# Giving each unit of split weights its own starting position within 128 bytes of SBUF

## The chip, the cores and the metric

The kernel runs on one core of one Trainium2 chip. The metric is the device time of one execution in microseconds. Before the change the median of three runs is 904.43 us (904.04 to 904.75). The profile comes from one execution of its own, which took 903.08 us; its span, from the first to the last instruction, is 901.3 us.

## The reference, cut to what matters

A decoder trunk of two layers works on 256 tokens of width 1024. All of it is float32.

```python
for l in range(DEPTH):
    y = hybrid_mixer(x, w_in[l], ...)          # three attention branches, gates, output projection
    x = layer_norm(DN_ALPHA * x + y, ln_g[l, 0], ln_b[l, 0])
    y = memory_cross_attention(x, mem, xa_w_q[l], xa_w_kv[l], xa_w_o[l])
    x = layer_norm(DN_ALPHA * x + y, ln_g[l, 1], ln_b[l, 1])
    y = jnp.square(jax.nn.relu(x @ mlp_w_up[l])) @ mlp_w_down[l]
    x = layer_norm(DN_ALPHA * x + y, ln_g[l, 2], ln_b[l, 2])
```

Nearly all of the arithmetic is products of activations (256 rows) with weight matrices that are read once from HBM.

## The kernel before, in words

**Split products.** Every large product is made from three matmuls in the type float32r. Each operand is split into a high part and a low part, and `mm3` (line 316) adds high times high, low times high and high times low into one PSUM tile. So each piece of a weight is used three times, twice through its high half and once through its low half.

**The weight stream.** All weights lie in HBM as one stream of units, each 128 partitions by 1024 float32. `load_to` (line 242) fetches a unit by DMA into one of five `raw` buffers. `split_piece` (line 254) then splits it in two pieces of 512 columns: ScalarE writes the high half (`hi`, line 266), VectorE subtracts it from the raw weight and writes the low half (`lo`, line 267). `pump`, which is called from every `tick` of the matmul loop, keeps up to four units split ahead of the one in use.

**Where the halves lie.** Units of three groups (`t1`, `ut`, `mem`; the list `IN_PAGES`) get their halves as `phi` and `plo` from a pool of pages. All other units get `whi` and `wlo` from the pool `wp`, six buffers for each name. In the built program the `whi` buffers begin at byte 80192 of each partition and every 4096 bytes after it, the `wlo` buffers at 104768 and every 4096 bytes after it. The activations `xhi` and `xlo` begin at 16512 and 24704; the pool of pages begins at 141632 in steps of 4096, and that of half pages (`hh`, `hl` of the MLP among them) at 129344 in steps of 2048. Counted modulo 128 bytes, `xhi` and `xlo` and all their slices begin at 0; `whi`, `wlo`, the pages and the half pages, and all their slices that a matmul reads, begin at 64.

**How TensorE reads them.** A matmul has a stationary operand of 128 by 128, which a weight load brings in, and a moving operand of 256 or 512 columns. Both are read from SBUF, and the weight load for the next matmul runs while the present one streams. Three uses matter here:

- `f_tile` (line 326): the weights are stationary (slices of 128 columns), and 256 columns of activations move. Used for most of the input projection, the gates, the branch projections and the MLP's first product.
- `product` in `mlp` (line 1116): the activations `hh` and `hl` are stationary, and 512 columns of the weights `whi` and `wlo` move.
- `t_chunk` (line 582): as `product`, with 512 or 256 columns of weights moving, for `t1`, `t2`, `mix`, `ut`, `xq` and `xv`.

```python
    def f_tile(self, out, unit, xT, kt=KT, off=0, cols=P):
        self.mm3(out, [(tuple(u[:, off + k * P:off + k * P + cols] for u in unit),
                        tuple(x[:, k, :] for x in xT)) for k in range(kt)])
```

```python
        def product(p, k, tb, ch, t):
            self.mm3(acc[tb][ch], [(tuple(y[:, k, tb * P:(tb + 1) * P] for y in hs[p]),
                                    tuple(v[:, 512 * ch:512 * ch + 512] for v in t))],
```

The functions that the change touches:

Of the kernel before, what the change touches and what calls it, by code (L numbers as in the profile page):

```python
# [11 lines left out]
F32R = mybir.dt.float32r  # L12
# [8 lines left out]
P = 128  # L21
# [29 lines left out]
def stream_groups():  # L51
    per = [("t1", 2), ("t1", 2), ("misc", 1), ("fq", 2), ("fk", 2), ("t2", 2), ("t2", 2), ("uq", 2),
           ("nq", 2), ("nq", 2), ("ncv", 2), ("nk", 2), ("w1", 2), ("w1", 2)]
    for j in range(4):
        per += [("gmf", 2), ("gmf", 2), ("brmf", 1)]
    per += [("gn", 2)] * 4 + [("brn", 2)] * 2
    per += [("mix", 2)] * 2 + [("mem", 2)] + [("mix", 2)] * 2
    per += [("xk", 2), ("xq", 2), ("xv", 2), ("xo", 2)]
    per += [("ut", 2), ("ut", 2)]
    for p in range(2, 16):  # L60
        per += [("up", 2), ("dn", 2)]
    per += [("dn", 2)] * 2
    return per
# [124 lines left out]
class Halves:  # L188


    def __init__(self, tiles):
        self.tiles = tiles
# [5 lines left out]
def r(ap):  # L198
    return ap.bitcast(F32)
# [30 lines left out]
class Kernel:  # L230
    def __init__(self, tc, a, out, scratch):
        self.tc, self.nc, self.a, self.out, self.scr = tc, tc.nc, a, out, scratch
        self.groups = [(l, n, k) for l in range(L) for n, k in stream_groups()]
        self.offs = np.concatenate([[0], np.cumsum([k for _, _, k in self.groups])])
        self.units = [(i, k) for i, (_, _, n) in enumerate(self.groups) for k in range(n)]
        self.raws, self.halves = {}, {}
        self.gi = self.next_load = self.next_piece = 0
        self.mv = {}
        self.side, self.work = [Side() for _ in range(NSIDE)], 0.0


# [12 lines left out]
    def split_piece(self):  # L254

        u, c = divmod(self.next_piece, 1024 // SPL)
        self.next_piece += 1
        self.load_to(u)
        if c == 0:
            if self.paged(u):  # L260
                self.halves[u] = (self.page([P, 1024], F32R, "phi"), self.page([P, 1024], F32R, "plo"))
            else:
                self.halves[u] = tuple(self.wp.tile([P, 1024], F32R, name=n, tag=n) for n in ("whi", "wlo"))
        sl = (slice(None), slice(c * SPL, c * SPL + SPL))
        hi, lo = self.halves[u]
        self.nc.scalar.activation(hi[sl], self.raws[u][sl], AF.Copy)  # L266
        self.nc.vector.tensor_sub(lo[sl], self.raws[u][sl], r(hi[sl]))  # L267
# [913 lines left out]
```

## Time and profile before

| What | Value |
|---|---|
| median of three runs | 904.43 us |
| profiled execution | 903.08 us |
| its span | 901.3 us |
| outside the span | 1.8 us |
| TensorE (PE) busy | 877.9 us, 97% |
| weight loads (PEld) busy | 798.0 us, 89% |
| VectorE (DVE) busy | 643.7 us, 71% |
| ScalarE (ACT) busy | 540.9 us, 60% |
| GpSimd (POOL) busy | 52.8 us, 6% |
| mean DMA rate | 178 GB/s |

Matmuls are pipelined, and the end of one in the records is modelled. So the busy time of one matmul (some 280 ns for 256 columns) is not what it costs in a stream; that is the distance from its start to the start of the next, and it is read from the timeline, as the distance of two rows' starts divided by the number of matmuls between them. At the full clock of 2.4 GHz 256 columns at one column a cycle are 106.7 ns, and 512 columns are 213.3 ns.

### The profile page before, as it was taken

Reading aid. Unit: us, or ns where it says so; the run is one execution under the profiler, and the core shown is the slowest. Engines: PE = TensorE matmul, PEld = TensorE weight load, DVE = VectorE, ACT = ScalarE, POOL = GpSimd, SP = SyncE. Lnnn points to the kernel's source line nnn. Section 1 sums busy time; section 2 is a strip of 40 time slices with the busy share of each in tenths; the row PEclk is TensorE's granted clock in tenths of the full one; section 3 lists DMA queues with packets and bytes.
Section 4 is the critical chain, followed back from the end, with each engine's and each line's share of the span. In section 5 each row is a group of like instructions: output and inputs, shape, how many; then the busy total and the mean of one; then the engine's idle time right before and its main releaser. Section 6 shows DMA issues by size and latency. Waiting matters only on the chain.

```text
span 901.3 us, 16105 instructions
## 1 busy us (share of the span) xinstructions
PE 877.9 (97%) x6034; PEld 798.0 (89%) x6034; DVE 643.7 (71%) x1411; ACT 540.9 (60%) x1173; POOL 52.8 (6%) x114
## 2 busy tenths in 40 slices
PE   8999999999999999999999999999999999999996
PEld 6999899998877999999889999999988689999994
DVE  5888898768886555555776989886778845555554
ACT  6777967556683444555656777675567545555551
POOL 1000000001211000000130000000021300000002
PEclk9999999999999999999999999999999999999998
DMA  9854645547553566666645435554667446666631
GB/s 330 264 184 146 207 159 158 160 148 275 181 201 118 187 194 192 190 188 190 209 123 179 143 118 178 178 160 139 194 210 252 165 123 187 190 196 188 191 95 47
DMA packets 46539, 160.80 MB, mean 178 GB/s; under 512 B 5941, under 2 KB 7381, under 8 KB 46334
## 3 DMA queue, kind: packets, MB, share of 16 engines
q1 hardware_dynamic: 46462, 159.78, 55.2%
q8 instruction: 47, 0.77, 0.3%
q14 instruction: 30, 0.25, 0.1%
HBM read 158.68 MB, written 1.07 MB: 177 GB/s over the span
## 4 chain that ended last, share of the span: by engine, by line
PE 86%; DVE 5%; POOL 3%; ACT 2%; issue 2%; DMA 1%; DVEq 0%; SPq 0%; POOLq 0%
PE mm L322 51%; PE S L322 14%; PE O L322 10%; DVE wlo L267 1%; PE S L744 1%; PE T L927 1%; POOL mv L476 1%; PE S L1050 1%; DVE xtok L450 1%; DVE xtok L486 1%; PE T L551 1%; PE O L561 1%; DVE xlo L341 1%; PE T L492 1%; DMA raw<-in_wst_dram 1%
## 5 line engine op out<-in xcount | busy, mean ns | idle before, releaser
L267 DVE TENSOR_TENSOR wlo<-raw,whi 128x512 fp32r<-128x512 f32 x524 | 341.0, 687 | 114.1 <-ACT whi L266 110.5
L266 ACT ACTIVATE whi<-raw 128x512 fp32r<-128x512 f32 x524 | 302.2, 624 | 145.1 <-issue 89.3
L322 PE MATMUL mm<-xhi,whi 128*128 128x256 f32 x1024 | 143.9, 282 | 0.1
L322 PE MATMUL mm<-xlo,whi 128*128 128x256 f32 x1024 | 143.8, 281 | 0.0
L322 PE MATMUL mm<-xhi,wlo 128*128 128x256 f32 x1024 | 142.7, 281 | 0.0
L322 PEld LDWEIGHTS mm<-xhi,whi 128*128 128x128 f32 x1024 | 131.8, 188 | 3.7 <-issue 0.7
L322 PEld LDWEIGHTS mm<-xhi,wlo 128*128 128x128 f32 x1024 | 130.4, 188 | 1.6 <-issue 0.3
L322 PEld LDWEIGHTS mm<-xlo,whi 128*128 128x128 f32 x1024 | 130.8, 188 | 1.1
L512 ACT ACTIVATE P<-sb,nm 128x128 f32<-128x128 f32 (+1 forms) x96 | 42.7, 445 | 16.5 <-DVE nm L510 16.1
L322 PE MATMUL S<-whi,hh 128*128 128x512 f32 x128 | 50.4, 394 | 0.0
L322 PE MATMUL S<-wlo,hh 128*128 128x512 f32 x128 | 50.1, 391 | 0.0
L322 PE MATMUL O<-whi,hh 128*128 128x512 f32 x128 | 50.0, 391 | 0.0
L322 PE MATMUL O<-wlo,hh 128*128 128x512 f32 x128 | 49.9, 390 | 0.0
L322 PE MATMUL O<-whi,hl 128*128 128x512 f32 x128 | 49.8, 389 | 0.0
L322 PE MATMUL S<-whi,hl 128*128 128x512 f32 x128 | 49.7, 389 | 0.0
L459 POOL TENSOR_SCALAR mv<-mv 128x1 f32<-128x1 f32 x36 | 9.0, 264 | 672.7 <-DVE xtok L450 671.7
L1125 DVE TENSOR_TENSOR tg<-tg 128x512 f32<-128x512 f32 x28 | 19.4, 692 | 38.4 <-ACT tg L1124 38.4
L1124 ACT ACTIVATE tg<-mm 128x512 f32<-128x512 f32 x28 | 16.7, 597 | 43.2 <-PE mm L322 43.2
L461 ACT ACTIVATE lnsq<-xtok,mv 128x512 f32<-128x512 f32 x24 | 17.3, 721 | 28.5 <-POOL mv L459 15.8
L267 DVE TENSOR_TENSOR plo<-raw,phi 128x512 fp32r<-128x512 f32 x40 | 26.0, 689 | 5.1 <-ACT phi L266 5.0
L322 PEld LDWEIGHTS S<-wlo,hh 128*128 128x128 f32 x128 | 24.0, 188 | 5.6
L322 PEld LDWEIGHTS O<-whi,hl 128*128 128x128 f32 x128 | 24.0, 188 | 5.1
(306 smaller groups left out, 1437.0 us busy)
## 6 DMA issues: line engine op xcount, KB each, us to landing
raw<-in_wst_dram SPq DMA_DIRECT2D x281, 512.0 KB, 3.9
lng<-in_lng_dram SPq DMA_DIRECT2D x6, 512.0 KB, 5.9
lnb<-in_lnb_dram SPq DMA_DIRECT2D x6, 512.0 KB, 5.8
wskew<-bias_scratch SPq DMA_DIRECT2D x4, 400.0 KB, 5.7
xt<-in_xT_dram SPq DMA_DIRECT2D x4, 256.0 KB, 4.1
xtok<-in_xtok_dram SPq DMA_DIRECT2D x1, 1024.0 KB, 6.8
out_dram<-xtok SPq DMA_DIRECT2D x4, 256.0 KB
raw<-in_wst_dram SPq DMA_DIRECT2D x2, 256.0 KB, 4.3
```

Source lines behind the costliest of these rows:

```text
L266: self.nc.scalar.activation(hi[sl], self.raws[u][sl], AF.Copy)
L267: self.nc.vector.tensor_sub(lo[sl], self.raws[u][sl], r(hi[sl]))
L322: mm(out, a[i], b[j], start=first and ps == 0 and k == 0, stop=last and ps == 2 and k == n - 1)
L341: nc.vector.tensor_sub(lo, src, r(hi))
L450: nc.vector.scalar_tensor_tensor(xs, xs, ALPHA, ac, op0=OP.mult, op1=OP.add, accum_out=mv[:, i:i + 1])
L461: nc.scalar.activation(sq, xs, AF.Square, bias=mv[:, 4:5], scale=1.0 / ROOT, accum_out=mv[:, 2 + i:3 + i])
L476: nc.gpsimd.tensor_scalar(col[9], col[8], col[8], col[7], op0=OP.mult, op1=OP.subtract)
L486: nc.vector.scalar_tensor_tensor(x[:, c], st["z"][:, c], col[11], gb[1][:, c], op0=OP.mult, op1=OP.add)
L492: nc.tensor.transpose(ps[:, k, :], x[:, 512 * i + k * P:512 * i + (k + 1) * P], self.ident)
L512: nc.scalar.activation(p_ap, t[:, :n], AF.Exp, bias=nmax, scale=-1.0, accum_out=sums)
L1124: nc.scalar.activation(t, ps, AF.Relu)
L1125: nc.vector.tensor_mul(t, t, t)
```

## The change

A counter `nwp` numbers the units that take their halves from the pool `wp`. Each such unit gets buffers of 1056 columns in place of 1024 (128 bytes more in each partition), and uses 1024 of them, beginning at the element `o = (5 * nwp + nwp // 4) % 32`. The high and the low half of a unit begin at the same `o`. Successive units run through all 32 positions. A position is 4 bytes, so of the 32 positions 16 are odd elements, 24 are no multiple of 16 bytes, and two (0 and 16) are multiples of 64 bytes.

```diff
-        self.mv = {}
+        self.mv, self.nwp = {}, 0
...
             if self.paged(u):
                 self.halves[u] = (self.page([P, 1024], F32R, "phi"), self.page([P, 1024], F32R, "plo"))
             else:
-                self.halves[u] = tuple(self.wp.tile([P, 1024], F32R, name=n, tag=n) for n in ("whi", "wlo"))
+
+                o = (5 * self.nwp + self.nwp // 4) % 32
+                self.nwp += 1
+                self.halves[u] = tuple(self.wp.tile([P, 1056], F32R, name=n, tag=n)[:, o:o + 1024] for n in ("whi", "wlo"))
```

The instructions of every engine, their order and what they wait for stay as they were. In the built program the `whi` and `wlo` buffers now lie 4224 bytes apart, and everything behind the pool `wp` lies 1536 bytes higher. Both are multiples of 128, so apart from `o` no operand changes its place modulo 128: `xhi` and `xlo` stay at 0, pages and half pages at 64, and `whi` and `wlo` are at 64 plus 4 times `o`.

## Rows read from the trace of the kernel before

**Rows 1.** The profile's page: busy times of the engines, the granted clock of TensorE in 40 slices, and the chain of work that ended last, by engine and by line.

```profile
PE 877.9 (97%) x6034; PEld 798.0 (89%) x6034; DVE 643.7 (71%) x1411; ACT 540.9 (60%) x1173; POOL 52.8 (6%) x114
...
PEclk9999999999999999999999999999999999999998
...
PE 86%; DVE 5%; POOL 3%; ACT 2%; issue 2%; DMA 1%; DVEq 0%; SPq 0%; POOLq 0%
PE mm L322 51%; PE S L322 14%; PE O L322 10%; DVE wlo L267 1%; PE S L744 1%; PE T L927 1%; POOL mv L476 1%; PE S L1050 1%; DVE xtok L450 1%; DVE xtok L486 1%; PE T L551 1%; PE O L561 1%; DVE xlo L341 1%; PE T L492 1%; DMA raw<-in_wst_dram 1%
```

**Rows 2.** What TensorE waited for in the whole span: engine and line, and what it waited for: us in total, times, the longest in us.

```profile
PE T L492 <- DVE xtok L486: 9.1, 10, 1.4
PE S L322 <- ACT xhi L340: 1.2, 2, 0.7
PE S L363 <- DVE zero L360: 1.2, 1, 1.2
PE O L561 <- ACT PT L553: 1.2, 3, 0.4
```

**Rows 3.** The chain that ended last in order of time, in the MLP of layer 0: start in us, us, what, how many. `mm` are the matmuls of `f_tile` with `whi` or `wlo` stationary, `S` and `O` those of `product` with `whi` or `wlo` moving.

```profile
327.27 5.66 PE mm L322 x48
332.93 1.39 PE S L322 x6
334.32 1.36 PE O L322 x6
335.69 1.36 PE S L322 x6
337.05 1.36 PE O L322 x6
```

**Rows 4.** Timeline of TensorE at the end of the branch projection of layer 0 and in the output projection behind it: start in us, us until the modelled end, engine, line, operation, out<-in, form, count. `on` is a page; it moves against `whi` or `wlo` as stationary in the first four rows, and `whi` or `wlo` moves against the page `mg` in the others.

```profile
204.78 0.64 PE L322 MATMUL mm<-onlo,whi 128*128 128x256 f32 x4
205.26 0.64 PE L322 MATMUL mm<-onhi,whi 128*128 128x256 f32 x4
205.74 0.64 PE L322 MATMUL mm<-onhi,wlo 128*128 128x256 f32 x4
206.22 0.64 PE L322 MATMUL mm<-onlo,whi 128*128 128x256 f32 x4
206.70 1.09 PE L322 MATMUL S<-whi,mg 128*128 128x512 f32 x4
...
208.09 1.07 PE L322 MATMUL S<-whi,mg 128*128 128x512 f32 x4
209.00 0.61 PE L322 MATMUL S<-wlo,mg 128*128 128x512 f32 x2
209.45 1.07 PE L322 MATMUL S<-whi,mg 128*128 128x512 f32 x4
210.36 0.61 PE L322 MATMUL S<-wlo,mg 128*128 128x512 f32 x2
210.81 1.07 PE L322 MATMUL S<-whi,mg 128*128 128x512 f32 x4
```

**Rows 5.** Timeline of TensorE, same columns, in the query projection of the cross-attention of layer 0: 256 columns of `whi` or `wlo` move, `xhi` or `xlo` is stationary. Four matmuls a row, without a gap between the rows.

```profile
239.10 0.62 PE L322 MATMUL mm<-wlo,xhi 128*128 128x256 f32 x4
239.55 0.62 PE L322 MATMUL mm<-whi,xhi 128*128 128x256 f32 x4
...
240.91 0.62 PE L322 MATMUL mm<-whi,xhi 128*128 128x256 f32 x4
```

**Rows 6.** Timeline of TensorE, same columns, at the start of layer 1 (group `t1`): 512 columns of the pages `phi` or `plo` move, `xhi` or `xlo` is stationary. Two matmuls a row; nine such rows from the first to the last that is shown.

```profile
451.82 0.63 PE L322 MATMUL S<-phi,xhi 128*128 128x512 f32 x2
452.29 0.63 PE L322 MATMUL S<-phi,xlo 128*128 128x512 f32 x2
...
456.02 0.63 PE L322 MATMUL S<-phi,xhi 128*128 128x512 f32 x2
```

**Rows 7.** Timeline of TensorE, same columns, in the gates of layer 0, just before it turns to the attention's small products: the same kind of matmul as the `mm` of rows 3.

```profile
141.07 0.73 PE L322 MATMUL mm<-xlo,whi 128*128 128x256 f32 x5
141.64 1.07 PE L322 MATMUL mm<-xhi,whi 128*128 128x256 f32 x8
142.54 0.39 PE L939 MATMUL O<-PT,nv 128*128 128x512 f32 x1
```

**Rows 8.** The matmuls of line 322 by their tiles: count, duration in ns (minimum/median/maximum), start of the first and the last in us, forms.

```profile
L322 PE MATMUL mm<-xhi,whi x1024: 276/279/388, 21.6 to 874.2; 128*128 128x256 f32 x171
...
L322 PE MATMUL S<-whi,hh x128: 389/389/402, 288.2 to 886.4; 128*128 128x512 f32 x128
...
L322 PE MATMUL mm<-onhi,whi x64: 278/283/290, 195.2 to 648.8; 128*128 128x256 f32 x64
...
L322 PE MATMUL S<-whi,mg x64: 389/389/397, 206.7 to 660.1; 128*128 128x512 f32 x64
```

**Rows 9.** The page's costliest groups: line, engine, operation, out<-in, forms, count, busy us, mean ns of one, idle time of the engine before them and what ended it. And, from the view of line 267, who waited for it in the whole span (us, times).

```profile
L267 DVE TENSOR_TENSOR wlo<-raw,whi 128x512 fp32r<-128x512 f32 x524 | 341.0, 687 | 114.1 <-ACT whi L266 110.5
L266 ACT ACTIVATE whi<-raw 128x512 fp32r<-128x512 f32 x524 | 302.2, 624 | 145.1 <-issue 89.3
```

```profile
  PEld mm L322: 0.7, 2
```

**Rows 10.** The instructions that read the tile `wskew` and write `biasq`, ScalarE (line 414): count, ns (minimum/median/maximum), first and last start, form. They read backwards from element 399 of the tile, an odd one.

```profile
L414 ACT ACTIVATE biasq<-wskew x4: 622/627/632, 91.0 to 97.9; 128x512 f32<-128x512 f32 x4
```

**Rows 11.** Busy time of the engines by stage: the stretch in us, its length, then PE, PEld, DVE, ACT, POOL, each with the number of instructions, the granted clock, the share of the DMA engines, GB/s.

```profile
50.00:135.00 85.00, 83.43 (x693) 80.35 (x692) 76.54 (x230) 65.65 (x176) 1.11 (x3) 1.00 0.54 172
...
266.00:452.00 186.00, 183.29 (x1137) 163.57 (x1136) 113.03 (x185) 95.63 (x175) 7.08 (x16) 1.00 0.59 182
```

## The prediction

> **What bounds the kernel now.** I read the page first: TensorE is busy for 97% of the span at the full clock, and the chain of work that ended last is TensorE for 86%, three quarters of it the matmuls of line 322 [rows 1]. Next I asked what TensorE waits for. The waits add up to some 14 us, the longest group being the transposes behind the layer norm (9.1 us), and no group of a microsecond names the halves that the change moves [rows 2]; weight loads waited for line 267 twice, 0.7 us together [rows 9]. So the conversion of weights is hidden, and the time is the sum of distances between the starts of matmuls. Only two things could reach the end: those distances, or a conversion so much slower that TensorE begins to wait.
>
> Then I read the distances themselves, because a matmul's busy time in the records says nothing on them. The reader is to see that matmuls with the same number of columns do not all keep the same distance:
>
> - 256 columns of `xhi` or `xlo` (position 0 modulo 128) against stationary `whi` or `wlo` (position 64): 48 in 5.66 us, 117.9 ns each [rows 3].
> - 256 columns of a page (64) against `whi` or `wlo` (64): 16 from 204.78 to 206.70, 120.0 ns each [rows 4].
> - 256 columns of `whi` or `wlo` (64) against `xhi` or `xlo` (0): 16 from 239.10 to 240.91, 113.1 ns each [rows 5].
> - 512 columns of `whi` or `wlo` (64) against `hh` or `mg` (64): in the MLP 24 in 1.39 + 3 x 1.36 = 5.47 us, 227.9 ns each [rows 3]; in the output projection 12 from 208.09 to 210.81, 226.7 ns [rows 4].
> - 512 columns of a page (64) against `xhi` or `xlo` (0): 18 from 451.82 to 456.02, 233.3 ns each [rows 6].
>
> The bare columns would be 106.7 and 213.3 ns. So every matmul carries 6 to 20 ns more, and how much goes with the relative position of its two operands, in opposite directions for the two widths: at equal positions 256 columns are slow and 512 columns fast. One more row shows that position does not settle it alone: the 13 matmuls from 141.07 to 142.54 are of the first kind and keep 113.1 ns [rows 7]. My reading is that the moving read and the weight load that runs beside it get in each other's way, at points that depend on where both stand.
>
> The Trainium skill says otherwise: by "SBUF — State Buffer", Who interferes with whom, TensorE has two independent read ports and never waits on anyone, and by "TensorE: Matmul & The Clock Gate", Part 2, loading the next weights takes nothing from the running matmul. By that rule a position could not matter and the sum would be zero; the 113.1, 117.9 and 120.0 ns for one width speak against it, though they do not prove that SBUF is where the reads meet. It stands as a rival below.
>
> **The change part by part.** The wider buffers, the shifted pools and the counter cost no instruction; all work and its order stay. What changes is the position of the weights in 3940 + 1104 matmuls, and in the 1048 conversions.
>
> No row shows a position between the two, nor any operand of a long matmul that begins off a multiple of 64 bytes. So I bound each kind by the distances that the rows show at the two relative positions (equal, and 64 apart), and take the mean of the two for units that run through all 32. Counts are from the groups of matmuls [rows 8], times layers and tiles as the code gives them:
>
> 1. `f_tile` on `xhi` and `xlo`: three groups of 1024 and 48 of `misc`, 3120. Now 117.9; mean of 117.9 and 120.0 is 118.95; +1.05 ns each, +3.3 us. Ends: all at 113.1 gives -15.0 us, all at 120.0 gives +6.6 us.
> 2. 512 columns of weights against half pages and pages: six groups of 128 in the MLP, 192 in `mix`, 48 in `xo`, 1008. Now 227.9; mean of 227.9 and 233.3 is 230.6; +2.7 ns each, +2.7 us. Ends: all at 226.7 gives -1.2 us, all at 233.3 gives +5.4 us.
> 3. 512 columns of weights against `xhi`, `xlo` (`t2`): 96, now taken as 233.3, becoming 230.6: -0.3 us.
> 4. 256 columns, weights stationary, against pages (`brn` 192, `brmf` 192, `uq` 84, `xk` 96): 564, now 120.0, becoming 118.95: -0.6 us; ends -3.9 and 0.
> 5. 256 columns of weights moving: `xq` 96 from 113.1 to 116.6, +0.3 us; `w1`, `xv` 160 from 120.0 to 116.6, -0.5 us.
>
> The sum is 3.3 + 2.7 - 0.3 - 0.6 + 0.3 - 0.5 = +4.9 us. All of it is on the path, because TensorE bounds nearly every stage [rows 1, 11].
>
> The conversions: ScalarE writes, VectorE reads and writes, from odd elements on half of the units. Nothing here shows such a write. Of reads, `biasq` is read from an odd element, backwards, in 627 ns [rows 10], against 624 ns for the aligned conversion of the same size [rows 9]: no cost. From below, I see no way in which a shifted start makes them shorter than the aligned conversion, so 0; from above, twice the time. I take 0, the nearest row. The cover is TensorE: in the MLP VectorE is busy for 113.0 of 186 us [rows 11], so 20% more on line 267 would vanish; from 50 to 135 us VectorE is busy for 76.5 of 85 us, so there about 10% more would begin to show.
>
> The Trainium skill has one more rule that speaks against the change: "SBUF — State Buffer", SBUF cachelines, gives lines of 16 bytes and a penalty for each step to a new line. A slice of 128 columns then covers 33 lines in place of 32 on 24 of the 32 positions. If TensorE paid a full line for it, 3.3 ns, the 5044 matmuls would cost three quarters of 16.6 us, an estimate of +12.5 us from that page. No row shows an unaligned slice. It bears on the fourth case below, and no number there hangs on it.
>
> The profiled execution took 903.08 us, of which 901.3 are span. 903.08 + 4.9 = 908.0. The median of the runs is 1.35 us above the profiled one, so the forecast against the median is 904.43 + 4.9 = 909.3; I say 909.
>
> **The cases.**
>
> - **Forecast: positions average out a little worse (0.38).** Both of the large kinds stand at the better of the two relative positions seen for their width outside the short stretches of rows 7, so spreading can lose more than it gains. 905 to 915, by the ends of terms 1 and 2 taken together (+6.6 and +5.4 us, less what terms 3 to 5 give).
> - **Rival 1, faster: the reads come apart (0.30).** Rows 7 show that the main kind runs at 113.1 ns for a stretch without any move of its operands, and rows 5 that a whole projection does. If starts off the 64-byte grid hold that rhythm, term 1 gives -15.0 us and term 4 -3.9 us; term 2 gives at most -1.2 us by the rows. That is 884.3 in full and 894.4 by half. For it: nothing in rows 3 to 7 is near the bare columns, so there is room. Against it: the rhythm of rows 7 is rare, the stream falls back to 117.9 after an interruption, and no row says which start brings it about.
> - **Rival 2, nothing (0.22).** The extra 11 ns are a matter of turn-taking inside TensorE and do not feel 4-byte steps, or gains and losses over the 32 positions cancel. 904.4, within 2 us. For it: the opposite signs for 256 and 512 columns.
> - **Rival 3, slower by more: odd starts slow the moving read (0.10).** Its place is `product`, `mix`, `xo` and `t2`, where weights move: 1104 matmuls, half of them from an odd element. Each 1% by which these are longer than 227 ns costs 552 x 2.27 ns = 1.25 us. It decides over the forecast from 4% on, at 10% the time is 917, and twice the time (a read that gets one element where it got two) would be +125 us, 1030. For it: TensorE takes more from SBUF per ns than any other engine here (512 columns in 227 ns, ScalarE in 624). Against it: the 627 ns of rows 10.
>
> **How the numbers follow.** What a measurement of this kernel can tell from no change is about 0.2%, 1.8 us: faster is below 902.6, slower above 906.2. Faster: rival 1, with a little of rival 2 at its lower edge, 0.31. Slower: most of the forecast (0.34), rival 3 and a little of rival 2, 0.45. The rest is no change, 0.24. The range for 8 in 10 reaches into rival 1 to somewhat more than its half, 891, and to rival 3 at a little over 10%, 921. The forecast's own range is 905 to 915.
>
> **What would show it right or wrong.** In the profile after, the number of matmuls and their order are as before, so the distances tell. The `mm` chain of 48 in the MLP should take different times from pair to pair, between 5.4 us (113 ns) and 5.8 us (120 ns), with a mean of 5.71, and the 24 behind it between 5.4 and 5.6 us, with a mean of 5.53. The matmuls of `t1`, which read no moved buffer, must stay at 233.3 ns; if they change too, positions modulo 128 are not what counts. If all pairs take the 5.66 and 5.47 us of before, rival 2 holds; if most take 5.43, rival 1; if units with an odd `o` stand out in the 512-column matmuls and not in the others, rival 3. Means of lines 266 and 267 away from 624 and 687 ns would show a cost of the shifted starts on the other engines; new waits of TensorE for line 267 would show that it is no longer hidden. The forecast is wrong from the ground up if the distances move but the time does not, since then something else than TensorE's stream sets the end.

## The result, and the profile after

The changed kernel takes 910.1 us (median of four runs, 909.0 to 910.9) beside 904.5 us of the kernel before: a ratio of 1.0076 with a 95% interval of 1.0062 to 1.0090. So the change makes the kernel slower by 0.76%. The forecast was 909.0 us.

The profiled execution took 910.92 us with a span of 909.1 us, 7.8 us longer than the span before. The profiled execution of before lies 1.35 us under its median and that of after 0.8 us over its own, so the two traces show some 2 us more than the medians do.

The page of the kernel after, with lines that answer to [rows 1] and [rows 9]. The `split_piece` lines 266 and 267 are 269 and 270 now, and `mm3` is line 325.

```profile
PE 885.9 (97%) x6034; PEld 802.3 (88%) x6034; DVE 643.9 (71%) x1411; ACT 541.0 (60%) x1173; POOL 52.3 (6%) x114
...
PEclk9999999999999999999999999999999999999999
...
PE 83%; DVE 6%; ACT 3%; POOL 3%; DMA 2%; issue 2%; DVEq 0%; POOLq 0%; SPq 0%; ACTq 0%
...
L270 DVE TENSOR_TENSOR wlo<-raw,whi 128x512 fp32r<-128x512 f32 x524 | 341.1, 686 | 121.7 <-ACT whi L269 119.4
...
L269 ACT ACTIVATE whi<-raw 128x512 fp32r<-128x512 f32 x524 | 302.6, 625 | 153.3 <-issue 93.9
```

TensorE has the same 6034 matmuls and the full clock (0.998 of it granted), and 8.0 us more of busy time. The conversions, half of which now begin at odd elements, take 686 and 625 ns, as before (687 and 624). The waits of TensorE, as in [rows 2] (engine and line, what it waited for: us in total, times, the longest):

```profile
PE T L495 <- DVE xtok L489: 8.8, 10, 1.3
PE O L564 <- ACT vx L1069: 1.3, 1, 1.3
```

No group names the halves, and the longest is 0.3 us shorter than before. What remains is the distances between starts. The chain in order of time in the MLP of layer 0, with the columns of [rows 3]:

```profile
306.44 5.63 PE mm L325 x48
312.07 1.42 PE S L325 x6
313.50 1.42 PE O L325 x6
314.91 1.39 PE S L325 x6
316.30 1.40 PE O L325 x6
317.70 5.69 PE mm L325 x48
...
357.17 1.44 PE S L325 x6
358.61 1.44 PE O L325 x6
```

Where before each set of six took 1.36 us once it had settled (227 ns a matmul), they now take 1.39 to 1.44 us in these lines (232 to 240 ns) and 1.36 to 1.44 in the whole MLP of layer 0, unlike from unit to unit; the sets of 48 take 5.55 to 5.78 us over both layers in place of 5.66. Two more stretches, from the timeline of TensorE (columns as in [rows 5] and [rows 6]): `xq` of the cross-attention, where the weights move, and `t1` of layer 1, which reads none of the buffers that the change shifts.

```profile
239.32 0.65 PE L325 MATMUL mm<-whi,xhi 128*128 128x256 f32 x4
239.81 0.65 PE L325 MATMUL mm<-whi,xlo 128*128 128x256 f32 x4
...
241.28 0.64 PE L325 MATMUL mm<-whi,xlo 128*128 128x256 f32 x4
...
455.56 0.63 PE L325 MATMUL S<-phi,xlo 128*128 128x512 f32 x2
...
459.29 0.63 PE L325 MATMUL S<-phi,xhi 128*128 128x512 f32 x2
```

`xq` keeps 122.5 ns (16 from 239.32 to 241.28), against 113.1 in [rows 5]. `t1` keeps 233.1 ns (16 from 455.56 to 459.29), against 233.3 in [rows 6].

A few rows are a small sample, so I took from each trace the start of every matmul of line 322 (325), formed the distance to the next start, left out breaks (over 175 ns for 256 columns, over 300 ns for 512), and took means by kind. "Weights still" means weights stationary; "pages" takes in half pages. These means, in ns, are what all experiments below are read by:

| Kernel | weights still, 256 of x move (3057) | 512 of weights move, pages still (995) | weights still, 256 of pages move (554) | `xq`: 256 of weights move, x still (92) | `t1`, `ut`: control (185) |
|---|---|---|---|---|---|
| before | 117.75 | 228.00 | 119.65 | 114.53 | 233.27 |
| after | 118.41 | 233.13 | 118.59 | 120.93 | 233.23 |
| all at 0 | 116.42 | 230.69 | 119.01 | 116.99 | 233.23 |
| all at 16 | 119.29 | 230.90 | 115.29 | 119.25 | 233.28 |
| moving alone | 116.26 | 233.18 | 119.11 | 121.17 | 233.07 |
| stationary alone | 118.45 | 230.64 | 118.24 | 116.07 | 233.57 |
| 64 mod 256 | 117.75 | 227.98 | 119.62 | 114.80 | 233.18 |
| two places | 116.29 | 227.39 | 118.61 | 114.49 | 233.14 |
| moving at 1 | 116.19 | 236.46 | 118.98 | 122.16 | 233.14 |
| moving at 3 | 116.03 | 229.91 | 118.99 | 118.81 | 233.16 |

All distances together, with the breaks left out in the same way, are 732.5 us before and 738.9 us after. So 6.4 of the 7.8 us lie in the distances.

### The profile page after: what moved, and what is told of

Its sections match the earlier page's. It is cut to its first block, busy times and chain, and to the rows that moved or that the text cites. A ratio compares the mean times of both kernels' runs of the same rounds, so it can differ in the third digit from the quotient of the medians.

```text
span 909.1 us, 16105 instructions
## 1 busy us (share of the span) xinstructions
PE 885.9 (97%) x6034; PEld 802.3 (88%) x6034; DVE 643.9 (71%) x1411; ACT 541.0 (60%) x1173; POOL 52.3 (6%) x114
## 4 chain that ended last, share of the span: by engine, by line
PE 83%; DVE 6%; ACT 3%; POOL 3%; DMA 2%; issue 2%; DVEq 0%; POOLq 0%; SPq 0%; ACTq 0%
PE mm L325 50%; PE S L325 14%; PE O L325 11%; DVE wlo L270 2%; PE T L930 1%; POOL mv L479 1%; PE S L747 1%; DVE xtok L453 1%; DVE xtok L489 1%; DMA raw<-in_wst_dram 1%; ACT whi L269 1%; DVE xlo L344 1%; PE T L554 1%; PE T L495 1%; POOL mv L478 1%
## 5 line engine op out<-in xcount | busy, mean ns | idle before, releaser
L325 PEld LDWEIGHTS O<-whi,hh 128*128 128x128 f32 x128 | 24.1, 188 | 5.7
```

The source lines that it names most:

```text
L325: mm(out, a[i], b[j], start=first and ps == 0 and k == 0, stop=last and ps == 2 and k == n - 1)
```

## The experiments

Each is made from the kernel after by another rule for `o`, unless said otherwise. MOV stands for the groups whose weights move: `t2`, `w1`, `mix`, `xq`, `xv`, `xo` and `dn`; `group` is the name of the unit's group. Times of before are from the same chip as the runs beside them; the first set ran on one chip, the second and third on another.

### First set: position, change of position, or the wider buffers

All units at one place, so that only the wider buffers and the shifted pools are left:

```diff
-                o = (5 * self.nwp + self.nwp // 4) % 32
+                o = 0
```

> The wide buffers stay, every unit begins at element 0, so all operands stand modulo 128 bytes as in the kernel before. Theory A (the cost of a matmul comes from the relative position of its own two operands) and theory B (the cost comes from the change of position between one unit and the next, which breaks a rhythm that TensorE has settled into; any constant position is as good as before): both 904.5 us, within 1 us, and the 24 matmuls of 512 columns behind an MLP pair in 5.47 us. Theory C (the shifted pools or the buffers' spacing of 4224 bytes matter, not the start in them): 909 to 911 us.

902.5 us beside 903.35: ratio 0.9992 (0.9979 to 1.0004), no change. But its parts did change. The chain in the MLP of layer 0:

```profile
324.23 1.39 PE S L325 x6
325.62 1.38 PE O L325 x6
327.00 5.66 PE mm L325 x48
332.66 1.37 PE S L325 x6
334.03 1.36 PE O L325 x6
...
338.12 5.66 PE mm L325 x48
343.78 1.39 PE S L325 x6
345.17 1.40 PE O L325 x6
```

One pair of units settles at 1.36 us and the next at 1.40; over the whole MLP it is one pair in three that keeps 1.36. Modulo 128 bytes nothing differs from before, so positions modulo 128 can't explain it. The buffers are 4224 bytes apart, 33 times 128, so every other one lies 128 bytes off modulo 256. The first two lines show something more: that unit stands at the place of the kernel before, but the unit ahead of it stands 128 bytes off. Over both layers such units keep 230.8 to 231.0 ns, against 227.1 ns where the unit ahead stands at the good place too: the distances go on varying for most of the unit (225 to 236 ns) before they settle at 227. The two places cancel in the time: 256 columns gain 3057 x 1.33 ns = 4.1 us, 512 columns lose 995 x 2.69 ns = 2.7 us.

All units 64 bytes further:

```diff
-                o = (5 * self.nwp + self.nwp // 4) % 32
+                o = 16
```

> Every unit begins at element 16, 64 bytes in. The weights then stand at 0 modulo 128: equal to xhi and xlo, 64 apart from pages and half pages. Theory A, by the distances of the kernel before: matmuls of 256 columns on xhi and xlo 120.0 in place of 117.8 ns (3120 times +2.2, +6.9 us), 512 columns against half pages 233.3 in place of 228.0 ns (1008 times +5.3, +5.3 us), t2 226.7 in place of 233.3 (-0.6 us), 256 columns against pages 117.8 in place of 119.7 (-1.1 us): about 915 us. Theory B: no change of position between units, so 904.5 us within 2 us.

908.37 us, ratio 1.0054 (1.0038 to 1.0071): slower, with no position off the 64-byte grid and none that changes other than by the buffers. Pages against weights became the fastest of all (115.29 ns) and x against weights among the slowest (119.29). So place alone has an effect, but not as relative position modulo 128 puts it: its 512 columns keep 230.9 ns, not 233.3, and the time is between the two that I had expected (915 and 904.5 us).

The stagger for the units whose weights move, and then for the others:

```diff
-                o = (5 * self.nwp + self.nwp // 4) % 32
+                o = (5 * self.nwp + self.nwp // 4) % 32 if group in MOV else 0
```

> Only the units whose weights move (t2, w1, mix, xq, xv, xo, dn) run through the 32 positions; all units whose weights are stationary begin at 0. From the distances in the profile after the change, 995 matmuls of 512 columns went from 228.0 to 233.1 ns (+5.1 us), 92 of 256 columns against xhi and xlo from 114.5 to 120.9 (+0.6 us). If the two parts of the change add up without touching each other: 910.1 us less the 2 us of the stationary part, so 908 us (907 to 909.5). If the rhythm of one kind depends on what ran before it (theory B), the stationary part slows down here too and the whole 910 us is reached, or nearly.

```diff
-                o = (5 * self.nwp + self.nwp // 4) % 32
+                o = 0 if group in MOV else (5 * self.nwp + self.nwp // 4) % 32
```

> The complement: only the units whose weights are stationary run through the 32 positions, those whose weights move begin at 0. If the parts add up: 3057 matmuls of 256 columns went from 117.75 to 118.41 ns (+2.0 us), 554 against pages from 119.65 to 118.59 (-0.6 us), so 906 us (905 to 907). The 24 matmuls of 512 columns behind an MLP pair should then stay at 5.47 us. If they rise towards 5.6 us although their operands stand as before, what ran before them counts (theory B).

Moving alone: 903.48 us, ratio 0.9997 (0.9985 to 1.0009). Stationary alone: 906.44 us, 1.0039 (1.0024 to 1.0054). The first misses the 907 to 909.5 us expected: I had taken 2 us off the changed kernel for its stationary part, as if those units went back to the kernel before, but at 0 they gain 4.1 us more on x, as in the run with all units at 0. In the table each half brings its own column to the value of after (233.18 and 118.45) and leaves the other where it is with all units at 0 (116.26 and 230.64). In sums of distances: all at 0 is 1.2 us under before; the moving units add 2.0 us to that, the stationary ones 5.8; together +6.6 us, against +6.4 in the trace of after. So the parts add up. With the stationary units staggered and the moving ones not, the `S` and `O` of the MLP are those of all units at 0, though the units of `mm` around them change place each time (230.64 and 230.69 ns in the table):

```profile
327.16 5.72 PE mm L325 x48
332.88 1.38 PE S L325 x6
334.26 1.36 PE O L325 x6
```

That speaks against the rival by which it is the change of position from one unit to the next that costs, as far as changes between the two kinds go. Between units of one kind a change does cost something, as the run with all units at 0 showed.

### Second set: modulo 256 bytes, and the place within 16 bytes

From the first set I formed a new theory: what counts is the relative position of the two operands modulo 256 bytes, and for the moving operand also where it begins within 16 bytes. Modulo 256, before has weights, pages and half pages at 64 and x at 128. In the trace of after, split by the element within 16 bytes at which moving weights begin, 512 columns keep 232.4, 236.8, 233.5 and 229.7 ns for elements 0 to 3 (228 to 271 distances each). For stationary weights the same split gives 118.4, 118.5, 118.1 and 118.6: nothing.

Wide buffers and shifted pools, but every unit back at 64 modulo 256:

```diff
-                o = (5 * self.nwp + self.nwp // 4) % 32
+                o = 32 * (0, 1, 0, 1, 1, 0)[self.nwp % 6]
```

> Wide buffers; units begin at 0 or at element 32 (128 bytes), by the buffer that they get, so that all weights stand at 64 modulo 256 bytes, as in the kernel before. Theory D: all distances return to those of the kernel before, 117.7 ns for 256 columns on xhi and xlo and 228.0 ns for 512 columns against half pages; in the run with every unit at 0 they were 116.4 and 230.7 ns. Time as before, ratio 1.000. If the period is longer than 256 bytes, or the pools' shift counts, the distances stay away from those of before.

903.81 us, ratio 0.9999 (0.9989 to 1.0010), and every mean of the table is that of before within 0.3 ns.

```profile
327.43 5.66 PE mm L325 x48
333.08 1.39 PE S L325 x6
334.48 1.36 PE O L325 x6
```

These are [rows 3] again. So the period is 256 bytes (128 is excluded by the run with all units at 0, a longer one by this run), and the width of the buffers and the shift of the pools cost nothing by themselves.

The stationary units at 192 and the moving ones at 64 modulo 256:

```diff
-                o = (5 * self.nwp + self.nwp // 4) % 32
+                o = 32 * ((0, 1, 0, 1, 1, 0)[self.nwp % 6] ^ (group not in MOV))
```

> Wide buffers; units with stationary weights begin at 192 modulo 256 bytes, units with moving weights at 64. Theory D (what counts is the relative position of the two operands modulo 256 bytes, and the element within 16 bytes): matmuls of 256 columns on xhi and xlo take the 115.5 ns that this relative position had in the earlier runs, in place of 117.7 (3057 times -2.2, -6.7 us); matmuls of 512 columns against half pages keep the 228.0 ns of the kernel before; 256 columns against pages 118.6 in place of 119.6 (-0.6 us). Together 7 us less than the kernel before, a ratio of 0.992. Theory A (modulo 128 bytes): no difference to the kernel before. Theory B (only changes of position between units cost): here the position changes between the two sorts of units, so the same or slower.

898.55 us beside 903.41: ratio 0.9944 (0.9930 to 0.9958), faster than both kernels. That is 4.9 us in place of the 7 expected: the mean of 256 columns of x came to 116.3 ns rather than the 115.5 hoped for. The timeline in the gates shows where it gains:

```profile
139.98 1.09 PE L325 MATMUL mm<-xlo,whi 128*128 128x256 f32 x8
140.90 1.07 PE L325 MATMUL mm<-xhi,whi 128*128 128x256 f32 x8
141.81 0.39 PE L942 MATMUL O<-PT,nv 128*128 128x512 f32 x1
```

16 matmuls from 139.98 to 141.81 are 114.4 ns each. Its MLP stayed as in [rows 3], as the chain shows:

```profile
325.37 5.66 PE mm L325 x48
331.03 1.37 PE S L325 x6
```

So the gain on x comes from the stretches outside the MLP's first product. The 512-column matmuls and the 256 columns of pages gave some 0.6 us each.

All moving units at element 1, constantly, and then at element 3:

```diff
-                o = (5 * self.nwp + self.nwp // 4) % 32
+                o = 1 if group in MOV else 0
```

> Wide buffers; units with moving weights all begin at element 1, all others at 0, so no change of position among the moving units. Theory D: 995 matmuls of 512 columns take 236 to 237 ns, as the units at elements 1, 5, 9 and so on do in the profile after the change, in place of 230.7 with every unit at 0: +5.5 us over that run, a ratio to the kernel before of 1.005. Theory B: a constant position, 230.7 ns, ratio 0.999.

```diff
-                o = (5 * self.nwp + self.nwp // 4) % 32
+                o = 3 if group in MOV else 0
```

> As the run with element 1, with element 3 for the units whose weights move. Theory D: 995 matmuls of 512 columns take 228.5 to 229.5 ns, 1.5 us less than with every unit at 0, ratio to the kernel before 0.997. Theory B: 230.7 ns, ratio 0.999. A theory by which any start off a multiple of 16 bytes costs: more than 230.7 ns, as with element 1.

Element 1: 907.24 us, ratio 1.0039 (1.0025 to 1.0053). Its chain in the MLP:

```profile
328.28 5.65 PE mm L325 x48
333.93 1.42 PE S L325 x6
335.35 1.42 PE O L325 x6
```

Element 3: 899.29 us, ratio 0.9952 (0.9934 to 0.9971). Its chain:

```profile
302.96 5.44 PE mm L325 x48
308.40 1.38 PE S L325 x6
...
313.94 5.65 PE mm L325 x48
```

With the position held constant, element 1 takes 236.5 ns (1.42 us for six) and element 3 only 229.9, where all units at 0 took 230.7. A stagger isn't needed for the loss. And element 3 is as odd as element 1, so it isn't oddness either. Nor does a start off a multiple of 16 bytes always cost: the kernel with element 3 is faster than the one with all units at 0. Its 229.9 ns lie just above the 228.5 to 229.5 expected and its time below the 0.997 expected, and one set of 48 in three takes 5.44 us here, where with all units at 0 none in this layer did, which I had not foreseen.

### Third set: the other operand

If relative position counts, moving x must do what moving the weights did. These are made from the kernel before; only the two tiles of the activations begin elsewhere, and the weights keep their place:

```diff
-        self.xhi = c.tile([P, KT, S], F32R, name="xhi")
-        self.xlo = c.tile([P, KT, S], F32R, name="xlo")
+        self.xhi, self.xlo = [c.tile([P, KT * S + 64], F32R, name=n)[:, 32:32 + KT * S].rearrange("p (k s) -> p k s", k=KT)
+                              for n in ("xhi", "xlo")]
```

> The weights' buffers are as in the kernel before, 1024 columns, all at 64 modulo 256 bytes; instead xhi and xlo begin 128 bytes later, at 0 modulo 256 in place of 128, with nothing else moved modulo 256. Theory D (relative position modulo 256 bytes): 256 columns of xhi and xlo against stationary weights stand as in the run with sorted positions, 115.2 to 116.3 ns in place of 117.75 (-4.5 to -7.8 us); 512 columns against half pages keep 228.0 ns; 512 columns of pages and of t2 against xhi and xlo take 229.5 in place of 233.3 ns (279 times, -1.0 us); xq 117.8 in place of 114.5 ns (+0.3 us). Together 5 to 8.5 us less than the kernel before, ratio 0.991 to 0.994. Theory A (modulo 128 bytes): ratio 1.000.

898.46 us beside 903.10: ratio 0.9949 (0.9935 to 0.9963), again faster than both kernels, from 128 bytes in the place of two tiles. The 4.6 us are a little less than the 5 to 8.5 expected. From the timeline of TensorE, the gates of layer 0 and `t1` of layer 1:

```profile
140.04 1.08 PE L322 MATMUL mm<-xlo,whi 128*128 128x256 f32 x8
140.96 1.07 PE L322 MATMUL mm<-xhi,whi 128*128 128x256 f32 x8
141.86 0.39 PE L939 MATMUL O<-PT,nv 128*128 128x512 f32 x1
...
449.91 0.62 PE L322 MATMUL S<-phi,xhi 128*128 128x512 f32 x2
450.37 0.62 PE L322 MATMUL S<-phi,xlo 128*128 128x512 f32 x2
...
454.03 0.62 PE L322 MATMUL S<-phi,xhi 128*128 128x512 f32 x2
```

The gates keep 113.8 ns (16 from 140.04 to 141.86), and `t1`, which had stayed at 233 ns in every kernel in which x and the pages kept their place, came to 228.9 (18 from 449.91 to 454.03; 230.0 is the mean over `t1` and `ut`). The MLP keeps its time here too, as the chain shows:

```profile
325.78 5.65 PE mm L322 x48
331.43 1.36 PE S L322 x6
```

The mean over all 256-column matmuls of x went from 117.75 to 116.36 ns, 4.2 us of the gain. It is a matter of shares: of some 3060 distances of this kind 155 were below 114.5 ns before, and 1085 are here (1212 with the weights at two places, 282 in the changed kernel), while most of the others stay at 117 to 119 ns.

Another 1.0 us came from 512 columns against pages, 228.0 to 227.0 ns, though none of their own operands moved: the first set behind each `mm` took 1.39 us in [rows 3] and takes 1.36 here. So what ran just before counts as well.

The same with x off the 16-byte grid, at element 29 and at element 26 in place of 32 (element 1 and element 2 within 16 bytes); the diffs are against the kernel just shown:

```diff
-        self.xhi, self.xlo = [c.tile([P, KT * S + 64], F32R, name=n)[:, 32:32 + KT * S].rearrange("p (k s) -> p k s", k=KT)
+        self.xhi, self.xlo = [c.tile([P, KT * S + 64], F32R, name=n)[:, 29:29 + KT * S].rearrange("p (k s) -> p k s", k=KT)
```

> As the run before it, with xhi and xlo 116 bytes later, at 244 modulo 256, an odd element and off the 16-byte grid. Theory D: the units at this relative position in the profile after the change took 114.7 ns for 256 columns (124 matmuls), so 3057 times -3.0, -9.2 us, if few units stand for all; 512 columns against xhi and xlo change by no more than 1 us in all. Ratio 0.990. If the few units there were lucky in what ran before them, 117 to 119 ns and a ratio near 1.

```diff
-        self.xhi, self.xlo = [c.tile([P, KT * S + 64], F32R, name=n)[:, 32:32 + KT * S].rearrange("p (k s) -> p k s", k=KT)
+        self.xhi, self.xlo = [c.tile([P, KT * S + 64], F32R, name=n)[:, 26:26 + KT * S].rearrange("p (k s) -> p k s", k=KT)
```

> As the run with 116 bytes, with 104 bytes (232 modulo 256). The units at this relative position took 115.2 ns for 256 columns (92 matmuls): -7.7 us, ratio 0.992. If position on the 64-byte grid is what keeps a rhythm stable: 118 to 120 ns, ratio 1 or above.

Element 29: 911.12 us, ratio 1.0088 (1.0073 to 1.0102), 120.6 ns for 256 columns of x. I had expected 114.7 from the trace of after, and that was a miss. Element 26: 915.80 us, ratio 1.0140 (1.0126 to 1.0154), 122.1 ns, beyond both the 115.2 and the 118 to 120 that I had named. The chain of the first in the MLP of layer 0, and then of the second:

```profile
319.01 5.76 PE mm L322 x48
324.77 1.37 PE S L322 x6
```

```profile
320.56 5.86 PE mm L322 x48
326.43 1.38 PE S L322 x6
```

The miss came from a relative position that I had read where the stationary operand was off the grid. A moving operand off the grid is another matter: here it costs 2.9 and 4.4 ns over the kernel before, while the `S` and `O` behind it, whose operands have not moved, stay at 1.36 to 1.38 us. None of the distances of x is below 114.5 ns in these two kernels.

The changed kernel once more, on the chip of this set (the parts of the first set ran on the other one):

> The changed kernel itself on the same chip as the parts. If the parts add up: wider buffers alone 0.9992, moving units on top of them +0.0005, stationary units on top of them +0.0047, so a ratio of 1.0044. If they don't, it comes out at the 1.0076 of the first measurement.

909.38 us, ratio 1.0067 (1.0053 to 1.0081). The loss is there again. By adding the ratios of the two halves of the first set I had expected 1.0044; in distances the halves do add up to within 0.7 us (+7.3 us here against +6.6), so the medians of that set, whose runs of one kernel spread over up to 5.6 us, are the weaker measure.

## Why the prediction was right, and where it was not

The likeliest case came about: positions average out a little worse, 910.1 us against 909.0. Its sign and size held, and so did the reason that the time is a sum of distances which go with the operands' positions. That the sum came out so near is in part luck: the rule that gave its terms (two places modulo 128, and the mean of the two) doesn't hold, and the two large terms missed in opposite directions. Step by step:

1. **256 columns of x against stationary weights** (forecast +1.05 ns, +3.3 us). Measured +0.66 ns, 3120 x 0.66 = +2.1 us. The rule behind it was wrong: positions count modulo 256, not 128, so the two rows that I averaged were two of at least four. On the 64-byte grid the runs give 117.1 to 117.8 ns at a relative position (moving less stationary) of 64, 115.8 to 116.4 at 192, 119.8 at 0 and 118.8 at 128; their mean is about 118.0. Before stood in the middle, not at the better end.
2. **512 columns of weights against pages** (forecast +2.7 ns, +2.7 us). This is the term that was mis-sized: +5.13 ns, 1008 x 5.13 = +5.2 us. "All at 233.3" was my upper end, and the mean of all units reached it. Both ends came from rows on the 64-byte grid. With all units at 0, which is on that grid, the cost is +2.7 ns; the rest is there only when moving weights begin off it, up to 236.5 ns at element 1. Here before did stand at the best of the four places (228.0 at a relative position of 0).
3. **`t2`** (-0.3 us): 233.33 to 231.73 ns, 96 x 1.6 = -0.15 us. The sign was right, the size half.
4. **256 columns of pages** (-0.6 us): 119.65 to 118.59 ns, 564 x 1.06 = -0.6 us. Right, though by two rules that happened to agree.
5. **256 columns of weights moving** (+0.3 and -0.5 us): `xq` went to 120.93, +6.4 ns x 96 = +0.6 us; `w1` stayed at 119.6 ns and `xv` went from 119.3 to 119.1, 0. Small, and half wrong.

The sum of what was measured is 2.1 + 5.2 - 0.15 - 0.6 + 0.6 = +7.1 us against a forecast of +4.9; the spans differ by 7.8, the medians by 5.6. In the MLP the 48 of a pair take 5.68 us on average and the 24 behind them 5.59, where the prediction had 5.71 and 5.53.

The steps that cost nothing held: the conversions at odd elements kept their 686 and 625 ns, nobody came to wait for line 270, and `t1` stayed at 233 ns. That last test was weaker than I took it for. I had put it as proof that positions modulo 128 are what counts, but x and the pages keep their places modulo 256 too, so it could not tell the two apart; all units at 0 did.

**Rival 1** (the reads come apart) has a true core: a rhythm of 113 to 114 ns exists and can be had for more stretches, as the gates with x moved show. The stagger hardly brings it about, and the full 15 us were nowhere to be had: with x moved or the weights at two places the MLP kept 5.65 or 5.66 us, and elsewhere only part of its sets came down to between 5.44 and 5.56. **Rival 2** (nothing) is excluded by the interval. **Rival 3** (odd starts slow the moving read) had the right place and the wrong property. Against all units at 0, element 1 costs 236.5 / 230.7 = 2.5% and element 3 gains 0.3%, both odd; element 2 of x, an even one, cost more than element 1 (122.1 against 120.6 ns).

By the Trainium skill, "SBUF — State Buffer", Who interferes with whom, TensorE's two reads stay out of each other's way. The runs don't bear out what the prediction drew from it, that a position could not matter: moving x alone by 128 bytes took `t1` from 233 to 229 ns and the gates to 114. Whether it is the two reads that meet, they don't show. The same page, SBUF cachelines, gave an estimate of +12.5 us for slices that cross into one more line of 16 bytes. The runs show no such cost on the stationary side (118.1 to 118.6 ns for all four elements). On the moving side there is an effect, but one that differs for elements 1, 2 and 3, which all touch one more line: in the trace of after element 3 keeps 229.7 ns, less than the 232.4 of element 0.

**What stays open.** Why 256 bytes, and which two reads meet, no run shows. Nor is it settled what picks the rhythm, though what ran before has a part in it: one position has 113.8 ns in the gates and 117.8 in the MLP of the kernel with x moved, as it had in [rows 3] and [rows 7]. Of term 1, some 0.4 ns above the mean of the four grid places are unexplained. Why element 3 is better than element 0 is open too. Element 2 of moving weights was not tried held constant, and no kernel combined the moved x with weights at two places.

## What to carry to other kernels

When matmuls with equal columns keep unequal distances from start to start, sort the distances by the positions of both operands before anything else, and find the period by moving one of them: here 128 bytes in the place of two activation tiles was worth 0.5%, for 512 bytes of SBUF a partition. Choose one good relative position for each kind of matmul, keep it from one unit to the next, and time a moving operand that begins off the 16-byte grid before you keep it (elements 1 and 2 cost here, element 3 did not); a stagger over all positions averages good places with bad ones and adds the cost of the elements that are slow. A mean of two seen positions is a forecast only if no third kind of place comes into play.

## What the hardware showed that was not expected

- The distance between matmuls goes with the relative position of moving and stationary operand modulo 256 bytes. 512 columns of weights against half pages: 228.0 ns at 0, 229.4 at 64, 232.1 at 128, 232.3 at 192. 256 columns of x against weights: 119.8, 117.1 to 117.8, 118.8 and 115.8 to 116.4 ns at the same four.
- What ran just before has a part too. At a relative position of 0, 512 columns keep 231 ns behind a unit at 128 and 227.1 behind one at 0 (all units at 0), and 228.0 ns in the kernel before but 227.0 with x moved, though their own operands stand the same in both.
- The moving operand's place within 16 bytes counts, that of the stationary one hardly does (118.1 to 118.6 ns). 512 columns held at element 1: 236.5 ns, at element 3: 229.9, at element 0: 230.7; 256 columns of x at element 1: 120.6, at element 2: 122.1, at element 0: 116.4.
- Matmuls of one kind at one place can run in either of two steady rhythms, about 113.5 or 117.8 ns for 256 columns, and often keep it through a whole stretch. A better place shows as a larger share of the faster one: 1085 of some 3060 distances with x moved, 155 before.
- ScalarE writes, and VectorE reads and writes, float32 from odd elements at the same speed: with half of the units at odd elements the means for 128x512 are 625 and 686 ns, against 624 and 687.
